# One S5 layer, four edits: state products over four quarters of TensorE, a contiguous tap table, whole-block turns, and layer-norm sums of one operand

## The chip, the cores and the metric

The kernel runs on one core of a Trainium2 chip. The metric is the time of one execution on the device, in microseconds. TensorE (PE) multiplies a stationary operand, loaded into its 128 by 128 array, with a moving operand whose columns stream through, and writes to PSUM; a matmul may use only half of the rows or columns of the array. VectorE (DVE), ScalarE (ACT) and GpSimd (POOL) work beside it, and SyncE (SP) issues the DMAs. Each engine takes its instructions in order.

## The reference

The program is a trunk of two layers over 1024 tokens of 1024 channels, in float32. Layer 0 is an RWKV-7 time mixer, layer 1 an S5 state-space layer; each is followed by a squared-ReLU MLP, and each of the four sub-layers by a layer norm of a scaled residual sum. Cut to what matters here:

```
def layer_norm(x, g, b):
    mu = mean(x);  var = mean(square(x - mu))
    return (x - mu) * rsqrt(var + LN_EPS) * g + b

def s5_mix(x, ...):            # 64 groups of 16 channels, 64 complex states each
    abar, bbar = discretised(a, log_dt, b)
    h[t] = abar * h[t-1] + bbar @ x[t]
    y[t] = real(c @ h[t]) + d * x[t]
    z = gelu(y) @ w_glu
    return z[:d] * sigmoid(z[d:])

for i in range(2):
    h = layer_norm(alpha * h + mixer_i(h))
    h = layer_norm(alpha * h + square(relu(h @ w1)) @ w2)
```

## The kernel before

The tokens are worked in two halves of 512 (H = 0 in the tiles hA, H = 1 in hB), each as eight tiles of 128 channels by 512 tokens. The dense products make up most of the time. Each weight tile is loaded (wraw, two buffers, L169), split into a high and a low part (whi on ScalarE, L148; wlo on VectorE, L149), and three matmuls of 512 columns (L188) make up one product. The two halves run against each other: while one is in its mixer, the dense products of the other half's MLP lie in between.

No order is written out around the change. A planner sets the order of the instructions of every engine when the program is built, from priorities, its own due times and the buffers that are free. So an edit in one place can move instructions elsewhere.

The S5 layer works eight tokens at a time (SL = 8), so that a half has NSC = 64 columns of states. The effect of the last tokens on the next ones is taken from a table of taps (tT, used as tt), the effect of the state from another (tC, used as tcm), and a third (tB, used as tb) brings inputs into the states. s5_tables builds the three into DRAM, at 1120 to 1270 us: for each of eight tiles f, VectorE and POOL expand the powers (L1133 to L1138), TensorE makes the taps (pk, L1151), ScalarE copies them into kpad, a buffer whose lower part holds zeros (L1155), and SP stores kpad into tT in two stores (L1159), each of which repeats the shifted taps for the eight steps.

s5(H, h) then runs for each half.

- Turn of the input, for four pairs of channel tiles f2: pu1 brings tokens onto partitions in 16 turns (L154 is a plain matmul with the identity, L156 a transpose), ScalarE copies them (u1), pu2 turns them once more per group of 16 channels (L1195), giving ug, and pbu brings them into the states hb (L1206).
- Scan: VectorE and POOL advance the states (L1216 to L1222).
- Outputs, again for four f2 (called rounds): the tap products (L1250, of ug with tt) and the state products (L1255, of hb with tcm) are summed in py, for the two parities par of the groups one after the other; ScalarE copies py into y1 (L1257), TensorE turns it back (pyt, L1263), VectorE adds the input (yg, one buffer, L1265), ScalarE takes the GELU (L1267), and SP stores to s_y (L1268). The tables of one round fill the four buffers of the tag tab.

In these products j, the tile in the pair, is the half of the array's columns; for the state products par is the half of its rows.

layer_norm is called seven times with the eight tiles h. Two partial sums are added up, TensorE sums over channels with a matrix of ones (pm, L865 and L866), VectorE subtracts the mean (L868), ScalarE squares and VectorE and POOL add the squares up in two sums sq0 and sq1 (L876), and pq sums both over channels (L880).

PSUM tiles come from four pools: pd (three, dense products), pl (one, tag l), pa (two, tag a) and pc (two, tag c).

Of the kernel before, what the change touches and what calls it, by code (L numbers as in the profile page):

```python
# [8 lines left out]
F32 = mybir.dt.float32  # L9
# [9 lines left out]
HT = 512  # L19
KT = 8  # L20
# [50 lines left out]
def trunk(ctx, tc, A):  # L71
# [90 lines left out]
    def wload(src, kt, n, key=None):  # L162

        step = 512 // n
        out = []
        for k0 in range(0, kt, step):
            kept = low.get((key, k0)) if key else None
            raw = wp.tile([128, step, n], F32, tag="wraw", name="wraw", bufs=2)
            SP.dma_start(raw, src[:, k0 : k0 + step])  # L169
# [12 lines left out]
        return out  # L182

    bulk, hops = [], []
    ST = getattr(nc, STE)
# [662 lines left out]
    def layer_norm(h, gi, H, split_out=True):  # L848
# [5 lines left out]
        def plt(name):  # L854
            return pl.tile([128, HT], F32, tag="l", name=name)
# [10 lines left out]
        PE.matmul(pm, ones_c, h[7], start=False, stop=True)  # L866
        for t in h:
            V.tensor_sub(t, t, pm)  # L868
        sa = [lt("sq0"), lt("sq1")]
        for k, t in enumerate(h):  # L870
            if k < 2:
                S.activation(sa[k], t, AF.Square)
            else:
                q = lt("sq", "m")
                S.activation(q, t, AF.Square)
                (G if k % 2 else V).tensor_add(sa[k % 2], sa[k % 2], q)  # L876
        pq = plt("pq")
        for t in range(4):
            for j in range(2):
                PE.matmul(pq[:, t : t + 1], sa[j][:, t * 128 : (t + 1) * 128], ones_c[:, 0:1], start=j == 0, stop=j == 1)  # L880
# [138 lines left out]

    SL = 8  # L1020
    NSC = HT // SL
    tT = dr.tile([KT, 128, 2, 512], F32, name="tT")
    tB = dr.tile([KT, 128, 4, 2, 128], F32, name="tB")
    tC = dr.tile([KT, 128, 4, 2, 128], F32, name="tC")

    def s5_tables():
# [75 lines left out]
        V.tensor_sub(ci, ci, tq)  # L1102
        V.tensor_mul(ci, ci, den)

        kpad = pp.tile([128, 16, 16, 4], F32, name="kpad")
        G.memset(kpad, 0.0)
        for f in range(KT):
            gs = slice(4 * f, 4 * f + 4)
            bc = pp.tile([128, 2, 2, 4, 16], F32, tag="bc", name="bc", bufs=1)
            SP.dma_start(bc, A["s5bc"][f])  # L1110
            bb = pp.tile([128, 2, 4, 16], F32, tag="bb", name="bb", bufs=1)
# [40 lines left out]
                                  ca[ps_, g2, ri, 0:8].rearrange("p t c -> p (t c)"), start=ri == 0, stop=ri == 1)  # L1152
            for par in range(2):
                ps_ = slice(64 * par, 64 * par + 16)
                S.copy(kpad[ps_, 8:].rearrange("p t c g -> p g (t c)"), p[ps_])  # L1155
            tv = tT[f].rearrange("(s c) two n -> two c s n", c=16)
            for par in range(2):
                src = kpad[64 * par : 64 * par + 16, 1:9].rearrange("p t c g -> p (t c g)")
                SP.dma_start(tv[par], bass.AP(src.tensor, src.offset, [src.ap[0], (64, SL), src.ap[1]]))  # L1159

            bs = pp.tile([128, 4, 2, 128], F32, tag="bs", name="bs", bufs=1)
            for hf in range(2):
# [10 lines left out]
    def s5(H, h):  # L1173
# [4 lines left out]
            V.tensor_copy(hb[:, :, :, 0], carry[0])  # L1178
        ug = []
        for f2 in range(4):  # L1180
            u1 = s5p.tile([128, 8, SL, 16], F32, tag="u1", name="u1", bufs=2)
            for s2 in range(2):
                p = pa.tile([128, 4, 128], F32, tag="a", name="pu1")
                for j in range(2):
                    src = h[2 * f2 + j].rearrange("p (c s) -> p c s", s=SL)
                    for s in range(4):
                        turn(p[64 * j : 64 * j + 64, s], src[:, :, SL - 1 - 4 * s2 - s], ident, j)
                S.copy(u1[:, :, 4 * s2 : 4 * s2 + 4].rearrange("p g s c -> p s g c"),
                       p.rearrange("p s (g c) -> p s g c", g=8))
            for j in range(2):  # L1190
                f = 2 * f2 + j
                ps_ = slice(64 * j, 64 * j + 64)
                p = pc.tile([128, HT], F32, tag="c", name="pu2").rearrange("p (g n) -> p g n", g=8)
                for g in range(8):
                    PE.transpose(p[:, g], u1[ps_, g].rearrange("p s c -> p (s c)"), ident[ps_, ps_])  # L1195
# [39 lines left out]
        for f2 in range(4):  # L1235
            y1 = s5p.tile([128, SL, 4, 2, 16], F32, tag="u1", name="y1", bufs=2)
            tabs = []
            for f in (2 * f2, 2 * f2 + 1):
                tt = s5p.tile([128, 2, 512], F32, tag="tab", name="tt", bufs=4)
                SP.dma_start(tt, tT[f])  # L1240
                tcm = s5p.tile([128, 4, 2, 128], F32, tag="tab", name="tcm", bufs=4)
                SP.dma_start(tcm, tC[f])
                tabs.append((f, tt.rearrange("p two (n g) -> p two g n", g=4), tcm))
            for par in range(2):
                qs = slice(64 * par, 64 * par + 64)
                p = pc.tile([128, HT], F32, tag="c", name="py").rearrange("p (g n) -> p g n", g=4)

                for g2 in range(4):
                    for j, (f, tv, tcm) in enumerate(tabs):
                        PE.matmul(p[64 * j : 64 * j + 64, g2], ug[f][:, 2 * g2 + par], tv[:, par, g2],  # L1250
                                  start=g2 == 0, stop=False, skip_group_check=True)
                for g2 in range(4):
                    for ri in range(2):
                        for j, (f, tv, tcm) in enumerate(tabs):
                            PE.matmul(p[64 * j : 64 * j + 64, g2], hb[qs, 4 * f + g2, ri, 0:NSC], tcm[qs, g2, ri],  # L1255
                                      start=False, stop=ri == 1, skip_group_check=True)
                S.copy(y1[:, :, :, par].rearrange("p t g c -> p g t c"), p.rearrange("p g (t c) -> p g t c", t=SL))  # L1257
            for j in range(2):
                f = 2 * f2 + j
                js = slice(64 * j, 64 * j + 64)  # L1260
                p = pa.tile([128, SL, NSC], F32, tag="a", name="pyt")
                for t in range(SL):
                    PE.transpose(p[:, t], y1[js, t].rearrange("p g r c -> p (g r c)"), ident[js, js])  # L1263
                y = s5p.tile([128, HT], F32, tag="yg", name="yg", bufs=1)
# [131 lines left out]
```

## Time and profile before

| | |
|---|---|
| median of three runs | 2739.15 us (2727.84 to 2743.22) |
| profiled execution | 2746.6 us, span 2744.8 us |
| mean granted TensorE clock | 0.961 of full speed |
| TensorE, VectorE, ScalarE, GpSimd busy | 95%, 66%, 42%, 23% of the span |
| building the S5 tables | about 1120 to 1270 us |
| S5 of the first half | about 1327 to 1545 us |
| S5 of the second half | about 1858 to 2075 us |

The profile is of one execution. A busy time is the time in which the engine had an instruction running. A row of a timeline gives start, length, engine, line and the number of instructions of that line in a row. A row of groups gives line, engine, operation, output from inputs, shape and count, then busy time in all and the mean of one in ns, then the idle time of the engine just before them and what ended it. For an fp32 matmul with a plain (not a transposing) operation the trace holds two records.

### The profile page before, as it was taken

How to read it: one execution, taken by the hardware profiler on the slowest of the kernel's cores; microseconds unless marked ns; L12 is line 12 of the kernel's file. 1: busy time of each engine (PE TensorE's matmuls, PEld its weight loads, DVE VectorE, ACT ScalarE, POOL GpSimd, SP SyncE). 2: the span in 40 equal slices, each digit the busy share in tenths (PEclk: the TensorE clock that was granted, in tenths of full speed). 3: DMA queues.
4: the chain of work that ended last, by engine and by line, in shares of the span. 5: the costliest groups of instructions: out<-in, count | busy, mean ns of one | idle time of the engine just before them, and what ended most of it. 6: DMA issues, size and time to landing. Idle time of an engine off the chain costs nothing.

```text
span 2744.8 us, 43807 instructions
## 1 busy us (share of the span) xinstructions
PE 2598.4 (95%) x16582; PEld 2089.9 (76%) x16582; DVE 1813.3 (66%) x3191; ACT 1154.8 (42%) x2038; POOL 630.6 (23%) x515
## 2 busy tenths in 40 slices
PE   7999979989899999989999999999999999999997
PEld 5778757678677777767876788778778887788886
DVE  7477677577786867997567553674855546755556
ACT  7455574544543333353532332434223324433334
POOL 3121542432442122342122000120220101210101
PEclk9989979999899999999999999999999999999998
DMA  4765455564223334545333533233343322333333
GB/s 146 235 214 175 151 164 156 178 203 142 81 86 88 93 92 148 141 129 163 100 112 127 174 95 100 81 96 112 103 164 110 96 96 81 119 96 96 96 96 100
DMA packets 215058, 345.90 MB, mean 126 GB/s; under 512 B 21184, under 2 KB 75584, under 8 KB 214848
## 3 DMA queue, kind: packets, MB, share of 16 engines
q1 hardware_dynamic: 214848, 343.10, 40.5%
q8 instruction: 131, 2.15, 0.3%
q14 instruction: 79, 0.65, 0.1%
HBM read 279.06 MB, written 63.96 MB: 125 GB/s over the span
## 4 chain that ended last, share of the span: by engine, by line
PE 44%; DVE 4%; issue 3%; DMA 1%; POOL 1%; ACT 1%; ACTq 0%; SPq 0%; DVEq 0%; POOLq 0%
PE d L188 39%; PE py L1250 1%; PE py L1255 1%; DVE wlo L149 1%; DMA wraw<-in_mw_dram 1%; PE pu L154 1%; PE pbu L1206 1%; POOL rl L975 1%; DVE hA L991 0%; DMA s_y<-yg 0%; DVE t L1218 0%; DVE hB L991 0%; ACT whi L148 0%; DVE sq L876 0%; PE pu L1195 0%
## 5 line engine op out<-in xcount | busy, mean ns | idle before, releaser
L148 ACT CAST whi<-wraw 128x512 fp32r<-128x512 f32 x668 | 413.5, 620 | 929.1 <-PE d L188 623.2
L149 DVE TENSOR_TENSOR wlo<-wraw,whi 128x512 fp32r<-128x512 f32 x668 | 500.6, 750 | 426.8 <-ACT whi L148 404.3
L188 PE MATMUL d<-qbuf,whi 128*128 128x512 f32 (+1 forms) x2112 | 657.0, 394 | 23.8 <-DVE hA L991 12.8
L188 PEld LDWEIGHTS d<-qbuf,whi 128*128 128x128 f32 x2112 | 391.8, 191 | 120.0 <-DVE hA L991 17.8
L188 PE MATMUL d<-qbuf,wlo 128*128 128x512 f32 (+1 forms) x1056 | 411.9, 392 | 10.7 <-DVE wlo L149 10.4
L975 POOL TENSOR_TENSOR rl<-rl 128x512 f32<-128x512 f32 x128 | 157.2, 1228 | 1094.5 <-ACT rl L974 1094.5
L188 PE MATMUL d<-oAh,whi 128*128 128x512 f32 (+1 forms) x960 | 390.9, 411 | 15.5 <-ACT ev L418 6.3
L188 PE MATMUL d<-oAl,whi 128*128 128x512 f32 (+1 forms) x960 | 387.5, 405 | 3.0 <-DVE oAl L149 2.8
L188 PE MATMUL d<-oAh,wlo 128*128 128x512 f32 (+1 forms) x960 | 386.5, 405 | 2.4 <-DVE wlo L149 2.3
L188 PE MATMUL d<-oBh,whi 128*128 128x512 f32 x704 | 279.2, 397 | 0.0
L188 PE MATMUL d<-oBh,wlo 128*128 128x512 f32 x704 | 278.7, 396 | 0.2 <-DVE wlo L149 0.2
L188 PE MATMUL d<-oBl,whi 128*128 128x512 f32 x704 | 277.1, 394 | 0.0
L188 PEld LDWEIGHTS d<-qbuf,wlo 128*128 128x128 f32 x1056 | 201.7, 191 | 56.5 <-DVE wlo L149 14.5
L188 PEld LDWEIGHTS d<-oAh,whi 128*128 128x128 f32 (+1 forms) x960 | 185.9, 194 | 62.2 <-ACT ev L418 8.4
L188 PEld LDWEIGHTS d<-oAh,wlo 128*128 128x128 f32 (+1 forms) x960 | 185.8, 194 | 44.4 <-DVE wlo L149 3.2
L188 PEld LDWEIGHTS d<-oAl,whi 128*128 128x128 f32 (+1 forms) x960 | 185.6, 194 | 43.1 <-DVE oAl L149 5.2
L991 DVE TENSOR_TENSOR hB<-hB,d 128x512 f32<-128x512 f32 (+1 forms) x256 | 165.0, 650 | 71.2 <-PE d L188 68.0
L991 DVE TENSOR_TENSOR hA<-hA,d 128x512 f32<-128x512 f32 x240 | 162.1, 682 | 64.4 <-PE d L188 62.1
L188 PEld LDWEIGHTS d<-oBh,wlo 128*128 128x128 f32 x704 | 132.9, 189 | 32.4 <-issue 2.0
L188 PEld LDWEIGHTS d<-oBl,whi 128*128 128x128 f32 x704 | 133.1, 189 | 29.9 <-issue 0.7
L188 PEld LDWEIGHTS d<-oBh,whi 128*128 128x128 f32 x704 | 133.1, 189 | 29.0 <-issue 1.2
L149 DVE TENSOR_TENSOR qbuf<-rl,qbuf 128x512 fp32r<-128x512 f32 x128 | 95.0, 742 | 73.5 <-ACT qbuf L148 73.5
(374 smaller groups left out, 3804.8 us busy)
## 6 DMA issues: line engine op xcount, KB each, us to landing
wraw<-in_mw_dram SPq DMA_DIRECT2D x520, 256.0 KB, 2.7
wraw<-in_glu_dram SPq DMA_DIRECT2D x64, 256.0 KB, 2.7
low<-wlo SPq DMA_DIRECT2D x52, 256.0 KB, 2.6
wlo<-low SPq DMA_DIRECT2D x52, 256.0 KB, 3.6
wraw<-in_wk_dram SPq DMA_DIRECT2D x32, 256.0 KB, 3.5
wraw<-in_wr_dram SPq DMA_DIRECT2D x32, 256.0 KB, 3.9
wraw<-in_wv_dram SPq DMA_DIRECT2D x32, 256.0 KB, 4.3
yl<-s_y SPq DMA_DIRECT2D x32, 256.0 KB, 3.1
```

The lines of the kernel that those rows point to most:

```text
L148: S.copy(hi, src)
L149: (e or V).tensor_sub(lo, src, hi.bitcast(F32))
L154: PE.matmul(out, x, idt, start=True, stop=True)
L188: bulk.append((PE.matmul(p, w, x, **kw).ins, x.shape[-1]))
L975: G.tensor_mul(r, r, r)
L991: V.tensor_add(z, z, p)
L1206: PE.matmul(p[qs, g2, ri], tb[:, g2, ri, qs], u[:, 2 * g2 + par], start=True, stop=True)
L1250: PE.matmul(p[64 * j : 64 * j + 64, g2], ug[f][:, 2 * g2 + par], tv[:, par, g2], start=g2 == 0, stop=False, skip_group_check=True)
L1255: PE.matmul(p[64 * j : 64 * j + 64, g2], hb[qs, 4 * f + g2, ri, 0:NSC], tcm[qs, g2, ri], start=False, stop=ri == 1, skip_group_check=True)
```

## The change

The lines of the changed kernel are some 6 to 20 higher than those before: the dense products are L196 and wraw's load L171; the tap products are L1262 (before L1250), the state products L1270 (L1255), the turn back L1280 (L1263), yg's store L1285 (L1268), the stores into tT L1170 (L1159).

The four quarters. One round now has two PSUM tiles, one per parity, from two pools (pc and pa), and the state products go through j and par in turn, so that four products in a row use the four quarters of the array. inorder ties each of them behind the one before. The turned outputs pyt move from the pool pa to pl.

The tap table. kpad and tT are laid out with the group g ahead of the taps, so that the columns of one group are contiguous (they stood 16 bytes apart). Each tile's taps go out in eight stores instead of two, and kpad is doubled.

The turns. pu1 now turns blocks of 128 tokens by 128 channels (eight transposes per f2, every fourth token a column); pu2 picks even and odd with a matrix sel of two interleaved halves of the identity, in 32 matmuls in place of 16 transposes.

The layer norms. The last tile is added on VectorE, so that pm is one matmul; sq0 and sq1 are added on VectorE, so that pq takes four matmuls and not eight.

```
+    sel = cp.tile([128, 2, 64], F32, name="sel")
+    V.tensor_copy(sel, ident.rearrange("p (n e) -> p e n", e=2))
...
+    def inorder(prods):
+        for x, y in zip(prods, prods[1:]):
+            tc.add_manual_dep(y.ins, x.ins.name, ...)
...
+        V.tensor_add(b2, b2, h[7])
         V.tensor_add(a, a, b2)
         pm = plt("pm")
-        PE.matmul(pm, ones_c, a, start=True, stop=False)
-        PE.matmul(pm, ones_c, h[7], start=False, stop=True)
+        PE.matmul(pm, ones_c, a, start=True, stop=True)
...
+        V.tensor_add(sa[0], sa[0], sa[1])
         pq = plt("pq")
         for t in range(4):
-            for j in range(2):
-                PE.matmul(pq[:, t : t + 1], sa[j][:, t * 128 : (t + 1) * 128], ones_c[:, 0:1], start=j == 0, stop=j == 1)
+            PE.matmul(pq[:, t : t + 1], sa[0][:, t * 128 : (t + 1) * 128], ones_c[:, 0:1], start=True, stop=True)
...
-    tT = dr.tile([KT, 128, 2, 512], F32, name="tT")
+    tT = dr.tile([KT, 128, 2, 4, 128], F32, name="tT")
...
-        kpad = pp.tile([128, 16, 16, 4], F32, name="kpad")
-        G.memset(kpad, 0.0)
+        kpads = [pp.tile([128, 4, 16, 16], F32, name=f"kpad{j}") for j in range(2)]
+        for kpad in kpads:
+            G.memset(kpad[:, :, 0:8], 0.0)
...
             for par in range(2):
-                src = kpad[64 * par : 64 * par + 16, 1:9].rearrange("p t c g -> p (t c g)")
-                SP.dma_start(tv[par], bass.AP(src.tensor, src.offset, [src.ap[0], (64, SL), src.ap[1]]))
+                for g2 in range(4):
+                    src = kpad[64 * par : 64 * par + 16, g2, 1:9].rearrange("p t c -> p (t c)")
+                    SP.dma_start(tv[par, g2], bass.AP(src.tensor, src.offset, [src.ap[0], (16, SL), src.ap[1]]))
...
-            for s2 in range(2):
+            for j in range(2):
                 p = pa.tile([128, 4, 128], F32, tag="a", name="pu1")
-                for j in range(2):
-                    src = h[2 * f2 + j].rearrange("p (c s) -> p c s", s=SL)
-                    for s in range(4):
-                        turn(p[64 * j : 64 * j + 64, s], src[:, :, SL - 1 - 4 * s2 - s], ident, j)
+                src = h[2 * f2 + j].rearrange("p (m s) -> p s m", s=4)
+                for s in range(4):
+                    PE.transpose(p[:, s], src[:, 3 - s], ident)
...
                 for g in range(8):
-                    PE.transpose(p[:, g], u1[ps_, g].rearrange("p s c -> p (s c)"), ident[ps_, ps_])
+                    for e in range(2):
+                        PE.matmul(p[64 * (1 - e) : 64 * (1 - e) + 64, g], u1[:, j, g].rearrange("p s c -> p (s c)"),
+                                  sel[:, e], start=True, stop=True)
...
+            pp = [r.tile([128, HT], F32, tag=t, name="py").rearrange("p (g n) -> p g n", g=4)
+                  for r, t in ((pc, "c"), (pa, "a"))]
+            ...
+            for g2 in range(4):
+                for ri in range(2):
+                    for j, (f, tv, tcm) in enumerate(tabs):
+                        for par in range(2):
+                            qs = slice(64 * par, 64 * par + 64)
+                            prods.append(PE.matmul(pp[par][64 * j : 64 * j + 64, g2], hb[qs, 4 * f + g2, ri, 0:NSC],
+                                                   tcm[qs, g2, ri], start=False, stop=ri == 1, skip_group_check=True))
+            inorder(prods)
...
-                p = pa.tile([128, SL, NSC], F32, tag="a", name="pyt")
+                p = pl.tile([128, HT], F32, tag="l", name="pyt").rearrange("p (t n) -> p t n", t=SL)
```

The planner's order in two places. A row gives line, operation, output from inputs, shape, and how many in a row. First TensorE in the outputs of the first half, in the kernel before: the end of one round's dense products (the d rows), the turn back of the round before (pyt), and the products of the next round.

```order
L188 MATMUL d<-oBh,wlo 128x512
L1250 MATMUL py<-tt,ug 64x128
L1263 MATMUL pyt<-ident,y_13970 128x64 x16
L1250 MATMUL py<-tt,ug 64x128 x7
L1255 MATMUL py<-tcm,hb 64x128
L1250 MATMUL py<-tt,ug 64x128 x5
L1255 MATMUL py<-tcm,hb 64x128 x15
L1250 MATMUL py<-tt,ug 64x128 x3
L1255 MATMUL py<-tcm,hb 64x128 x16
L188 MATMUL d<-oBh,whi 128x512
```

The same place in the changed kernel:

```order
L1280 MATMUL pyt<-ident,y_13958 128x64 x8
L1262 MATMUL py<-tt,ug 64x128 x14
L1270 MATMUL py<-tcm,hb 64x128 x13
L1280 MATMUL pyt<-ident,y_13958 128x64 x8
L1270 MATMUL py<-tcm,hb 64x128 x19
L1262 MATMUL py<-tt,ug 64x128 x2
L196 MATMUL d<-qbuf,whi 128x512 x2
```

The sixteen turns back of one round stood together and are now two times eight, the second amid the next state products; and the first two tap products of the round that follows stand directly behind the last state product, ahead of the round's dense products.

Second, SP's queue while the tables are built, before:

```order
L169 DMA wraw<-in_wo_dram 128x512
L1168 DMA tB<-bs 128x1024
L1144 DMA tC<-ca 1024x1x128
L169 DMA wraw<-in_wo_dram 128x512 x2
L1159 DMA tT<-kpad 16x8x512 x2
L1110 DMA bc<-in_s5bc_dram 128x256
```

The changed kernel there:

```order
L171 DMA wraw<-in_wo_dram 128x512
L1154 DMA tC<-ca 1024x1x128
L171 DMA wraw<-in_wo_dram 128x512 x2
L1170 DMA tT<-kpad_12861 16x8x128 x8
L1120 DMA bc<-in_s5bc_dram 128x256
```

Two stores per tile have become eight, in a row, between the loads of weights (wraw).

More of the change, by code (lines that the diff above doesn't have):

```diff
@@ L1239, in s5 @@
                 tt = s5p.tile([128, 2, 512], F32, tag="tab", name="tt", bufs=4)
-                SP.dma_start(tt, tT[f])
+                SP.dma_start(tt, tT[f].rearrange("p two g n -> p two (g n)"))
                 tcm = s5p.tile([128, 4, 2, 128], F32, tag="tab", name="tcm", bufs=4)
                 SP.dma_start(tcm, tC[f])
-                tabs.append((f, tt.rearrange("p two (n g) -> p two g n", g=4), tcm))
-            for par in range(2):
[L1245 to L1257, printed above, removed]
@@ new lines, in s5 @@
+                tabs.append((f, tt.rearrange("p two (g n) -> p two g n", g=4), tcm))
+            pp = [r.tile([128, HT], F32, tag=t, name="py").rearrange("p (g n) -> p g n", g=4)
[3 more added lines that the diff above has]
+                    for j, (f, tv, tcm) in enumerate(tabs):
+                        PE.matmul(pp[par][64 * j : 64 * j + 64, g2], ug[f][:, 2 * g2 + par], tv[:, par, g2],
+                                  start=g2 == 0, stop=False, skip_group_check=True)
@@ new lines, in s5 @@
+            prods = []
+            for g2 in range(4):
+                for ri in range(2):
+                    for j, (f, tv, tcm) in enumerate(tabs):
+                        for par in range(2):
+                            qs = slice(64 * par, 64 * par + 64)
+                            prods.append(PE.matmul(pp[par][64 * j : 64 * j + 64, g2], hb[qs, 4 * f + g2, ri, 0:NSC],
+                                                   tcm[qs, g2, ri], start=False, stop=ri == 1, skip_group_check=True))
@@ L1258, in s5 @@
+            inorder(prods)
+            for par in range(2):
+                S.copy(y1[:, :, :, par].rearrange("p t g c -> p g t c"), pp[par].rearrange("p g (t c) -> p g t c", t=SL))
             for j in range(2):
```

13 lines of the change are left out of this document (7 added, 6 removed).

## The prediction

> **What bounds the kernel now.** I read the engine totals and the chain of waits on the page, then the tables of busy time by stretch, then single stretches instruction by instruction.
>
> ```profile
> PE 2598.4 (95%) x16582; PEld 2089.9 (76%) x16582; DVE 1813.3 (66%) x3191; ACT 1154.8 (42%) x2038; POOL 630.6 (23%) x515
> PE 44%; DVE 4%; issue 3%; DMA 1%; POOL 1%; ACT 1%; ACTq 0%; SPq 0%; DVEq 0%; POOLq 0%
> ```
>
> TensorE is busy for 95% of the span, and the chain that ended last runs mostly over it; all other engines together are some 10%. Only 146 us of the 2744.8 us span have no matmul running (2744.8 − 2598.4). So TensorE time taken out of a stretch where it never idles comes off the end, unless something else takes its place. The next tables show the stretches that the change touches; columns are us, busy time (and count) of PE, PEld, DVE, ACT, POOL, the granted clock, the DMA share and GB/s.
>
> ```profile
> 1180.00:1200.00 20.00, 15.93 (x88) 11.78 (x86) 19.65 (x28) 9.03 (x14) 8.75 (x8) 0.96 0.53 128
> 1330.00:1405.00 75.00, 75.00 (x616) 60.56 (x615) 33.02 (x49) 30.24 (x53) 6.91 (x6) 1.00 0.38 119
> 1405.00:1480.00 75.00, 67.35 (x286) 51.23 (x285) 65.96 (x112) 20.06 (x34) 23.22 (x13) 0.97 0.29 89
> 1480.00:1545.00 65.00, 65.00 (x547) 49.40 (x546) 30.90 (x42) 23.02 (x38) 8.68 (x5) 0.99 0.64 219
> ```
>
> The S5 of the first half has three parts: turning the input (1330 to 1405), the scan (to 1480) and the outputs (to 1545). In the first and the last TensorE is busy for the whole stretch: dense products of the other half fill every gap. In the scan VectorE is the busiest engine. The second half's S5 repeats this around 1860 to 2075. The row of 1180 to 1200 stands for the building of the S5 tables: there VectorE works 19.65 of 20 us, and TensorE has 4 us of slack.
>
> **State products and tap products.** Rows of the output stretch, start, length, engine, line:
>
> ```profile
> 1481.22 3.55 PE L1255 MATMUL py<-tcm,hb 64*64 64x128 f32 x64
> 1494.38 2.01 PE L1250 MATMUL py<-tt,ug 128*64 128x128 f32 x16
> 345.90 0.71 PE L596 MATMUL pA<-AR,KB 64*128 64x128 f32 x8
> L1255 PE MATMUL py<-tcm,hb 64*64 64x128 f32 x512 | 32.5, 275 | 0.0
> L1250 PE MATMUL py<-tt,ug 128*64 128x128 f32 x256 | 40.4, 408 | 0.0
> L1166 PE MATMUL pb<-ident,bp 128*128 128x128 f32 x64 | 11.8, 290 | 4.9 <-DVE bp L1138 3.3 <-DVE bp L1135 1.4
> ```
>
> The trace has two records for each fp32 matmul, which I call passes. One L1255 pass lasts 275 ns, and 64 take 3.55 us, far less than 64 times that: passes go in pairs, the two column halves beside each other, (3.55 − 0.275) / 31 = 106 ns from pair to pair. The change puts four quarters in a row. If the two row halves overlap as well, 64 passes take 16 such steps and not 32; the 512 passes of the eight f2 rounds (four a half) lose 128 × 0.106 = −13.6 us. That row halves can overlap is seen in L596: eight passes, alternating between two row halves and two PSUM tiles, in 0.71 us; one after the other, 106 ns apart, they would need 7 × 0.106 + 0.27 = 1.01 us. The four quarters at once are in no row: the bounds are 0 (row halves do not overlap in this shape; a loss I exclude, since the same passes are issued) and −13.6. Since the new code, as L596, gives the row halves a PSUM tile each, I take −13.6.
>
> A tap pass (L1250) lasts 408 ns where passes of 128 columns otherwise last 275 to 290, and 16 take 2.01 us, that is 8 pairs (2.01 − 0.408) / 7 = 229 ns apart where L1255's need 106. What differs is the moving operand: a column every 16 bytes before, contiguous after. 128 pairs × (0.229 − 0.106) = −15.7; the other bound is 0, if the stride is not the cause. I take −15.7, since contiguous operands of 128 columns in the other two rows agree.
>
> **Turns.**
>
> ```profile
> 1327.37 1.03 PE L156 MATMUL pu<-ident,hA 128*64 128x128 f32 x8
> 1328.34 2.19 PE L154 MATMUL pu<-ident,hA 128*64 128x128 f32 x16
> 1330.46 0.73 PE L188 MATMUL d<-qbuf,whi 128*128 128x512 f32 x2
> ...
> 1331.26 0.62 PE L188 MATMUL d<-qbuf,whi 128*128 128x512 f32 x2
> 1331.72 0.39 PE L188 MATMUL d<-qbuf,wlo 128*128 128x512 f32 x1
> 1331.95 0.61 PE L188 MATMUL d<-qbuf,whi 128*128 128x512 f32 x2
> ...
> 1337.99 1.01 PE L1195 MATMUL pu<-ident,u 64*128 64x64 f32 x16
> 1338.94 0.50 PE L188 MATMUL d<-oBh,wlo 128*128 128x512 f32 x1
> 1343.73 2.09 PE L1206 MATMUL pbu<-ug,tb 128*64 128x64 f32 x64
> L156 PEld LDWEIGHTS pu<-ident,hA 128*64 128x64 f32 x32 | 3.8, 133 | 1.0
> L1166 PEld LDWEIGHTS pb<-ident,bp 128*128 128x128 f32 x64 | 7.9, 143 | 9.3 <-DVE bp L1138 4.7 <-ACT whi L148 1.7 <-issue 1.3
> ```
>
> First turn, per f2: 8 transposes and 8 matmuls (16 passes) from 1327.37 to 1330.46, 3.09 us. After: 8 whole transposes. At L156's pitch (1328.34 − 1327.37) / 8 = 0.121 us that is 0.97 us, and with 0.2 us for the change of shape 1.2: −1.9, times eight −15. They now load 128 columns and at a stride of 16 bytes, which no row has; L156 loads 64 at 32 bytes, as quickly (133 ns) as L1166 loads contiguous columns (143 ns). Bounds: −9.6 if the pitch doubled, −16. Second turn: 16 transposes in 0.95 us become 32 matmuls, 64 passes of L1206's shape, whose row gives 64 in 2.09 us: 8 × (2.02 − 0.95) = +8.6. The shape is L1206's, so ± 1. (Three dense products from 1331.26 to 1331.95 give 0.23 us each, used below.)
>
> The Trainium skill ("SBUF — State Buffer", section "Door 1: The DMA port swizzle") says that an access which leaves its 16-byte line each time pays a penalty. The tap row agrees (408 against 275 ns); the rule would double the new whole-block loads too, and the sum would be 5.4 us smaller, while L156's load at 32 bytes shows none, so the measurement decides.
>
> **Layer norms.**
>
> ```profile
> 1761.58 1.95 PE L880 MATMUL pq<-ones_c,sq 128*128 128x1 f32 x16
> L880 PE MATMUL pq<-ones_c,sq 128*128 128x1 f32 x112 | 16.5, 271 | 3.0 <-DVE sq L876 2.8
> L868 DVE TENSOR_TENSOR hA<-hA,pm 128x512 f32<-128x512 f32 x32 | 19.5, 679 | 0.7 <-PE pm L866 0.7
> L876 DVE TENSOR_TENSOR sq<-sq,sq 128x512 f32<-128x512 f32 x21 | 21.7, 1035 | 0.0
> L876 POOL TENSOR_TENSOR sq<-sq,sq 128x512 f32<-128x512 f32 x21 | 29.5, 1406 | 36.5 <-ACT sq L875 36.5
> ```
>
> Seven calls (112 passes / 16). The sums of squares lose 8 of 16 passes: (1.95 − 0.27) / 15 = 0.112 us each, −0.90. The mean loses one matmul of 512 columns, two passes at four times 106 ns: −0.85. Together −1.75 × 7 = −12.2. VectorE gets two more adds, 2 × 7 × 0.68 to 1.04 us = +10 to +15 on its own account. The second also makes VectorE wait for POOL's last add (1.4 us), with the mean's 8 subtractions and the next products' splits behind it. TensorE waits for the sums 3.0 us in all seven calls now, since dense products of the other half lie beside them; the adds lengthen that chain by 1.4 to 3.5 us a call and the shorter sums give 1.8 back. I take +3; bounds 0 and +12 (1.7 a call).
>
> **New waits in the outputs.**
>
> ```profile
> 1489.60 1.01 PE L1263 MATMUL pyt<-ident,y 64*128 64x64 f32 x16
> ...
> 1532.87 1.01 PE L1263 MATMUL pyt<-ident,y 64*128 64x64 f32 x16
> 1490.35 1.17 DVE L1265 SCALAR_TENSOR_TENSOR yg<-hA,pv,pyt 128x512 f32<-128x512 f32 x1
> 1494.35 1.19 DVE L1265 SCALAR_TENSOR_TENSOR yg<-hA,pv,pyt 128x512 f32<-128x512 f32 x1 [2.82 <-DMA s_y<-yg]
> L1257 ACT COPY y<-py 128x512 f32<-128x512 f32 x16 | 9.4, 586 | 33.8 <-PE py L1255 23.1 <-POOL t L1220 10.6
> DMA to landing us min/median/max: 3.8/4.4/6.2
> ```
>
> The last row is of the table tT (all its transfers). Two things come nearer to TensorE. First, the turned output goes to a pool of one buffer: the second eight transposes stand amid the next state products and need VectorE's sum of the first eight to be done, and the next f2 needs the second sum, which waits for yg's store (2.82 us above, one buffer). 4.0 us lie between the two sums above; between the transposes in the new order lie at most 14 tap and 13 state matmuls (1.5 + 0.7 us) and, next, 18 dense ones (4.1 us). Second, in the new order two tap products of the next f2 stand right behind the last state product, and their table's load can start only when the current taps are over, that is 32 state matmuls (1.75 us) and 8 transposes (0.5 us) earlier. A load takes 4.4 us, so TensorE waits 4.4 − 2.3 = 2.1 us, in the last two rounds of each half (the first two have their buffers early): 4 × 2.1 = +8. Before, 21 dense products (4.8 us) lay in between. With the sum's wait uncovered as well, 2 us more in each of eight rounds, it is +24; the lower bound is +3, loads at 3.8 us and half of it hidden.
>
> **Tables.**
>
> ```profile
> L1159 SPq DMA_DIRECT2D tT<-kpad x16: 320/362/1264, 1128.6 to 1268.9; - x16
> SPq L169 <- DVE wlo L149: 65.4, 28, 5.6
> L1155 ACT COPY kpad<-pk 16x512 f32<-16x512 f32 x16 | 17.1, 1072 | 6.3 <-PE pk L1151 6.1
> ```
>
> Each tile's two stores become eight: 6 × 0.362 = +2.2 us on SP's queue, 17 us for eight tiles, ahead of weight loads (wraw, two buffers). In 1120 to 1270 SP itself waited 65.4 us for a free wraw buffer, so most is hidden; if that cover were gone it would be +17 and more. I take +4, bounds 0 and +17. The copy ahead of the stores gets a contiguous target (1072 ns now, 586 ns in L1257's row for as much data a partition), off the path. The doubled kpad and the one copy of sel I cost at nothing: VectorE's queue at the start and POOL's have slack (23% busy).
>
> **Sum.** −13.6 − 15.7 − 15 + 8.6 − 12.2 + 3 + 8 + 4 = −33 us. The profiled execution took 2746.6 us (span 2744.8), which would become about 2714; it lies 7.4 us above the median of the three runs, 2739.15, so against the median I predict 2706 us. 0.5%, about what these runs can tell from no change, is 13.7 us: faster means below 2725.5, slower above 2752.8.
>
> **Rivals.**
> Row halves do not overlap: state products keep 106 ns a pair; L596 speaks against it, its different shape for it. 2706 + 14 = 2720.
> The stride is not the tap pass's cost: 2706 + 16 = 2722. The equal 275 to 290 ns of both other rows speak against it.
> The outputs are paced by something else than TensorE: a round ((1532.87 − 1489.60) / 3 = 14.4 us) has four table loads of 512 KB, two yg stores and the chain through one pyt buffer, with a DMA share of 0.64 already. If the round stays at its length, the 29 us of products come back as idle time: −33 + 29 − 8 (the wait counted above) = −12, so 2727, and up to 2740 with waits of the upper bounds.
> Slower: the 64 stores hold the weight loads back. SP works its queue in order, so a store that waits for ACT's copy or for an earlier transfer holds wraw behind it, and TensorE has only two of them in hand while VectorE is full. To reach 2752.8 the wait must eat the gain and 14 more, 47 us, that is 6 us a tile beyond the 0.5 in the sum; the stores' own issue is 2.2, so each tile must also wait for about one landing (4.4 us). The 65.4 us that SP spends waiting speak against it.
>
> **How the numbers follow.** Forecast, 0.48, alone 2693 to 2720 (the bounds of turns, norms and waits). No overlap 0.12, no gain by contiguity 0.05, outputs paced by others 0.15, stores in the way 0.10, and 0.10 for the order changing elsewhere, either way. The range reaches from 2688 (waits at their lower bounds, −9, and 8 of run to run spread) to 2738, which holds the first three cases and most of the fourth and leaves out 0.18. Faster: 0.48 + 0.11 + 0.05 + 0.03 + 0.04 = 0.71; slower 0.07 + 0.03 = 0.10; the rest 0.19.
>
> **What would show it.** State products: 64 passes in about 1.8 us instead of 3.55. Taps: passes near 280 ns, 16 in 1.1 us. First turns: eight in 1.0 us; second: 64 in 2.0. The norms' sums: 8 passes in 1.0. TensorE idle at the first tap products of a round, about 2 us, released by the load of tt. TensorE busy about 2550 us. I am wrong if the four quarters still take 106 ns a pair, if the idle time in the outputs is above 15 us, or if TensorE idles more than now (4 of 20 us) while the tables are built.

## The result, and the profile after

The changed kernel took 2709.23 us (median of four runs, 2705.1 to 2714.34), the kernel before 2737.76 on the same occasions: a ratio of 0.9901, 95% interval 0.9875 to 0.9926, or 20 to 34 us less; the difference of the medians is 28.5 us where 33 were forecast. Medians leave out executions that were disturbed as a whole, such as one of 6511.5 us of the kernel with the old tap table. The profiled execution has a span of 2707.5 us. Engine totals and the chain that ended last, from its page, and the chain of a second execution of the same kernel:

```profile
PE 2541.4 (94%) x16768; PEld 2059.2 (76%) x16768; DVE 1830.7 (68%) x3206; ACT 1144.4 (42%) x2038; POOL 622.4 (23%) x516
PE 62%; DVE 18%; DMA 8%; issue 5%; ACT 5%; POOL 2%; SPq 0%; ACTq 0%; DVEq 0%; POOLq 0%
PE 43%; DVE 9%; DMA 4%; issue 2%; ACT 1%; POOL 0%; SPq 0%; ACTq 0%; DVEq 0%; POOLq 0%
```

TensorE is busy 57.0 us less (2598.4 − 2541.4), the span is 37.3 us shorter, so some 20 us of new idle time have come. The shares of the chain can't be compared: they add up to 100% here, to 59% in the second execution and to 54% in the kernel before, so the chain was followed over different parts of the span. VectorE's 18% and 9% are of one and the same kernel. The outputs of the first half, as a timeline and then as groups, and below them TensorE's busy time in the outputs of the first and of the second half:

```profile
1454.50 1.98 PE L1270 MATMUL py<-tcm,hb 64*64 64x128 f32 x64
1462.74 1.96 PE L1262 MATMUL py<-tt,ug 128*64 128x128 f32 x28
1470.02 1.11 PE L1262 MATMUL py<-tt,ug 128*64 128x128 f32 x4 [2.42 <-DMA tt<-tT]
...
1484.49 1.12 PE L1262 MATMUL py<-tt,ug 128*64 128x128 f32 x4 [2.56 <-DMA tt<-tT]
L1270 PE MATMUL py<-tcm,hb 64*64 64x128 f32 x512 | 17.7, 274 | 0.0
L1262 PE MATMUL py<-tt,ug 128*64 128x128 f32 x256 | 22.4, 284 | 9.2 <-DMA tt<-tT 9.2
1453.00:1511.00 58.00, 53.02 (x530) 42.58 (x529) 29.76 (x35) 22.21 (x39) 9.57 (x6) 0.91 0.66 231
1970.00:2025.00 55.00, 50.42 (x531) 40.27 (x530) 27.65 (x35) 19.89 (x36) 10.56 (x7) 0.97 0.60 206
```

64 state passes take 1.98 us, before 3.55: (1.98 − 0.274) / 15 = 114 ns for four. A tap pass lasts 284 ns, before 408; 14 pairs in a row are (1.96 − 0.284) / 13 = 129 ns apart, before 229. And TensorE waits 2.42 and 2.56 us for a table, at the place and for the reason that the order had shown. The last two rows give 5.0 + 4.6 = 9.6 us of idle time in the two output stretches, where the kernel before had none. The turns and the norms' sums, and four contiguous blocks turned in a row in the kernel before (L1166):

```profile
1324.94 1.11 PE L1198 MATMUL pu<-ident,hA 128*128 128x128 f32 x8
1325.81 0.48 PE L196 MATMUL d<-oBh,wlo 128*128 128x512 f32 x1
1331.04 2.08 PE L1205 MATMUL pu<-sel,u 128*64 128x64 f32 x64
1749.44 0.95 PE L888 MATMUL pq<-ones_c,sq 128*128 128x1 f32 x8
L1198 PEld LDWEIGHTS pu<-ident,hA 128*128 128x128 f32 x32 | 5.0, 206 | 0.5
1132.86 0.60 PE L1166 MATMUL pb<-ident,bp 128*128 128x128 f32 x4
```

Eight whole-block turns take 0.87 us up to the next product (predicted 1.2, before 3.09); the second turns 2.08 us, as predicted.

More new idle time lies around the layer norms. Three stretches without any S5 work, between the tables and the first S5, between the two S5, and after the second to the last norms, in the kernel before and then in the changed one (columns as in the prediction):

```profile
1272.00:1330.00 58.00, 57.14 (x267) 46.40 (x267) 43.81 (x66) 25.37 (x43) 12.32 (x10) 1.00 0.41 132
1536.00:1860.00 324.00, 322.45 (x1425) 262.57 (x1424) 192.00 (x288) 120.35 (x206) 47.80 (x43) 1.00 0.32 96
2063.00:2677.00 614.00, 610.02 (x2662) 497.79 (x2661) 347.54 (x525) 213.58 (x363) 74.50 (x69) 0.99 0.33 99
```

```profile
1235.00:1323.00 88.00, 81.91 (x355) 65.96 (x354) 63.24 (x94) 38.45 (x67) 22.17 (x16) 0.98 0.34 116
1511.00:1842.00 331.00, 324.05 (x1422) 264.20 (x1421) 197.16 (x295) 120.93 (x206) 48.51 (x44) 1.00 0.29 95
2025.00:2640.00 615.00, 608.11 (x2664) 496.91 (x2663) 353.27 (x534) 216.01 (x368) 76.07 (x71) 1.00 0.30 99
1253.68 1.24 ACT L150 CAST whi<-wraw 128x512 fp32r<-128x512 f32 x2 [9.46 <-DMA wraw<-in_mw_dram]
1254.35 0.50 PE L196 MATMUL d<-oAh,whi 128*128 128x512 f32 x1 [4.23 <-ACT whi L150]
```

Length less TensorE's busy time gives 0.9 + 1.6 + 4.0 = 6.4 us before and 6.1 + 7.0 + 6.9 = 19.9 after: 13.5 us more. The first stretch is not alike in the two (58 and 88 us), and 4.2 of its 6.1 us are one wait for a weight tile whose load came late (the last two rows); the other two stretches are alike and went from 5.5 to 13.8 us. What a norm looks like from VectorE and TensorE, timeline of the changed kernel:

```profile
1743.40 0.68 DVE L151 TENSOR_TENSOR wlo<-wraw,whi 128x512 fp32r<-128x512 f32 x1
1744.01 1.27 DVE L999 TENSOR_TENSOR hB<-hB,d 128x512 f32<-128x512 f32 x2
1745.20 0.68 DVE L885 TENSOR_TENSOR sq<-sq,sq 128x512 f32<-128x512 f32 x1
1745.81 0.67 DVE L999 TENSOR_TENSOR hB<-hB,d 128x512 f32<-128x512 f32 x1
1744.73 0.73 PE L196 MATMUL d<-qbuf,whi 128*128 128x512 f32 x2 [0.95 <-DVE hB L999]
```

VectorE works without a gap there; its queue holds the norm's adds, the splits of weights (wlo) and the sums that take dense products out of PSUM (hB, L999). TensorE's next dense product waits 0.95 us for such a sum. The new add (L885) stands in that same queue.

### The profile page after: what moved, and what is told of

Read it like the earlier page. It is cut to its first block, busy times and chain, and to the rows that moved or that the text cites. A ratio compares the mean times of both kernels' runs of the same rounds, so it can differ in the third digit from the quotient of the medians.

```text
span 2707.5 us, 44238 instructions
## 1 busy us (share of the span) xinstructions
PE 2541.4 (94%) x16768; PEld 2059.2 (76%) x16768; DVE 1830.7 (68%) x3206; ACT 1144.4 (42%) x2038; POOL 622.4 (23%) x516
## 4 chain that ended last, share of the span: by engine, by line
PE 62%; DVE 18%; DMA 8%; issue 5%; ACT 5%; POOL 2%; SPq 0%; ACTq 0%; DVEq 0%; POOLq 0%
PE d L196 55%; DVE wlo L151 3%; PE pA L604 2%; DMA wraw<-in_mw_dram 1%; DMA yl<-s_y 1%; DVE hA L999 1%; DMA s_y<-yg 1%; ACT whi L150 1%; DVE t L1229 1%; DMA ldsg<-s_sg 1%; DVE sq L884 1%; DVE hB L999 1%; PE pbu L1217 1%; PE pu L1205 1%; DVE xh L649 1%
## 5 line engine op out<-in xcount | busy, mean ns | idle before, releaser
L196 PE MATMUL d<-qbuf,whi 128*128 128x512 f32 (+1 forms) x2112 | 656.4, 393 | 31.4 <-DVE hA L999 15.2
L196 PEld LDWEIGHTS d<-qbuf,whi 128*128 128x128 f32 x2112 | 391.5, 191 | 126.9 <-DVE hA L999 23.4
L196 PE MATMUL d<-qbuf,wlo 128*128 128x512 f32 (+1 forms) x1056 | 409.5, 390 | 9.3 <-DVE wlo L151 9.1
L196 PE MATMUL d<-oAh,whi 128*128 128x512 f32 (+1 forms) x960 | 391.4, 411 | 21.9 <-ACT ev L426 6.5
L983 POOL TENSOR_TENSOR rl<-rl 128x512 f32<-128x512 f32 x128 | 145.1, 1133 | 1090.4 <-ACT rl L982 1071.3
L196 PE MATMUL d<-oAl,whi 128*128 128x512 f32 (+1 forms) x960 | 386.4, 404 | 1.1 <-DVE oAl L151 1.1
L196 PE MATMUL d<-oAh,wlo 128*128 128x512 f32 (+1 forms) x960 | 385.8, 404 | 1.0 <-DVE wlo L151 1.0
L196 PE MATMUL d<-oBh,wlo 128*128 128x512 f32 x704 | 278.4, 396 | 1.5 <-DVE wlo L151 1.5
L196 PE MATMUL d<-oBh,whi 128*128 128x512 f32 x704 | 279.8, 397 | 0.0
L196 PE MATMUL d<-oBl,whi 128*128 128x512 f32 x704 | 275.8, 392 | 0.0
L196 PEld LDWEIGHTS d<-qbuf,wlo 128*128 128x128 f32 x1056 | 201.2, 191 | 54.0 <-DVE wlo L151 12.8
L196 PEld LDWEIGHTS d<-oAh,whi 128*128 128x128 f32 (+1 forms) x960 | 185.8, 194 | 67.5 <-ACT ev L426 8.6
L196 PEld LDWEIGHTS d<-oAh,wlo 128*128 128x128 f32 (+1 forms) x960 | 185.9, 194 | 42.4 <-DVE wlo L151 2.0
L196 PEld LDWEIGHTS d<-oAl,whi 128*128 128x128 f32 (+1 forms) x960 | 186.2, 194 | 39.8 <-DVE oAl L151 2.2
L999 DVE TENSOR_TENSOR hB<-hB,d 128x512 f32<-128x512 f32 (+1 forms) x256 | 165.1, 652 | 65.8 <-PE d L196 62.7
L999 DVE TENSOR_TENSOR hA<-hA,d 128x512 f32<-128x512 f32 x240 | 162.4, 682 | 45.6 <-PE d L196 43.5
L196 PEld LDWEIGHTS d<-oBh,wlo 128*128 128x128 f32 x704 | 132.9, 189 | 33.4 <-DVE wlo L151 2.1
L196 PEld LDWEIGHTS d<-oBl,whi 128*128 128x128 f32 x704 | 132.8, 189 | 29.1 <-issue 0.2
L196 PEld LDWEIGHTS d<-oBh,whi 128*128 128x128 f32 x704 | 133.0, 189 | 28.5 <-issue 0.8
```

What stands on the lines that cost most here:

```text
L196: bulk.append((PE.matmul(p, w, x, **kw).ins, x.shape[-1]))
L983: G.tensor_mul(r, r, r)
L999: V.tensor_add(z, z, p)
```

## The experiments

All times are medians; each set ran beside the kernel before, and ratios are to that kernel. Two runs of the changed kernel gave 2709.23 and 2712.97. The sets ran on different chips, so the distances of medians from these two are rough. By ratios, against 0.9902 (the mean of the changed kernel's two), the run with row halves one after the other, the old tap table, the old turns and the old norms lie 6, 7, 10 and 17 us above it, and the intervals of the first two overlap the changed kernel's.

**The changed kernel again**

> The changed kernel unaltered, beside the others of this set: 2709 to 2712 on the chip where the kernel before takes 2738 to 2741. It says how far medians of equal kernels lie apart.

2712.97 us, ratio 0.9903 (0.9887 to 0.9919). Medians of one kernel lie up to 4 us apart, so differences below some 5 us say nothing here.

**Row halves one after the other**

```
-                    for j, (f, tv, tcm) in enumerate(tabs):
-                        for par in range(2):
+            for par in range(2):                # outermost
+                for g2 ... for ri ... for j ...
```

> The changed kernel with the state products of one parity after the other, so that only pairs of column halves stand in a row; the two PSUM tiles and all else stay. If row halves overlap and TensorE's own work sets the time, 64 passes take 3.5 us again instead of 2.0 and the kernel takes 13.6 us more than 2709, about 2723. Rival: the outputs are paced by the table loads; the products before each round's first taps are then 1.75 us longer and the wait of 2.2 to 2.6 us for tt shrinks by as much in four rounds, so only 13.6 - 7 = 7 us more, about 2716. If row halves did not overlap, no difference: 2709.

2721.08 us, ratio 0.9923 (0.9905 to 0.994): 8 to 12 us above the changed kernel by medians. Timeline and groups, and last a row of another line in the kernel before, used further down:

```profile
1461.59 3.34 PE L1270 MATMUL py<-tcm,hb 64*64 64x128 f32 x64
1479.08 0.65 PE L1262 MATMUL py<-tt,ug 128*64 128x128 f32 x4 [1.69 <-DMA tt<-tT]
L1270 PE MATMUL py<-tcm,hb 64*64 64x128 f32 x512 | 28.0, 273 | 0.0
L1262 PE MATMUL py<-tt,ug 128*64 128x128 f32 x256 | 22.8, 284 | 7.2 <-DMA tt<-tT 7.2
421.08 1.71 PE L596 MATMUL pA<-AR,KB 64*128 64x128 f32 x16
```

The order of the passes alone makes 3.34 us of 1.98: the four quarters do run at once. (With the row halves the two PSUM tiles also come one after the other here, so this run does not say which of the two the overlap needs.) Busy time of the state products is 10.3 us more (28.0 − 17.7), and the wait for tt is 2 us less, between the two theories: part of the gain of the quarters is lost to waiting for the tables.

**The tap table as before**

```
-    tT = dr.tile([KT, 128, 2, 4, 128], F32, name="tT")
+    tT = dr.tile([KT, 128, 2, 512], F32, name="tT")
...  (one kpad [128, 16, 16, 4], two stores a tile)
```

> The changed kernel with the tap table as before: group last, columns 16 bytes apart, two stores a tile, one kpad. If the stride costs, tap passes are 408 ns again and the eight rounds take 15.7 us more; the six stores a tile fewer give back what they cost (4 by the prediction): about +12, 2721. Rival: the eight stores cost as much as the contiguous reads gain: 2709. Second rival: the stride is not the cause, tap passes stay near 284 ns: about 2705.

2724.18 us, ratio 0.9926 (0.9905 to 0.9946): 11 to 15 us above the changed kernel by medians, 7 by ratios. This agrees with the stride, but alone does not show it, and no tap pass was read from a trace of this kernel. The other traces say it more plainly: a tap pass lasts 408 ns on the mean in the three other kernels with the old table (the kernel before, and that kernel with eight stores and with the new norms, below), and 275 to 299 in the changed kernel and all its variants with the contiguous one.

**The turns as before**

```
-                src = h[2 * f2 + j].rearrange("p (m s) -> p s m", s=4)
-                for s in range(4):
-                    PE.transpose(p[:, s], src[:, 3 - s], ident)
+                    turn(p[64 * j : 64 * j + 64, s], src[:, :, SL - 1 - 4 * s2 - s], ident, j)
...  (and pu2 as 16 transposes)
```

> The changed kernel with the first and second turn of the input as before. By the trace the first turn lost 20.1 us of TensorE's time and the second gained 8.6, so +11.5 us, about 2721. Rival: these savings were given back in the scan behind them, where VectorE is the busiest engine: 2709.

2723.44 us, ratio 0.9938 (0.9921 to 0.9956): 10 to 14 us more, the first theory. The turns' gain was not given back. (The groups of the first turn add up to 28.3 us before and 9.8 after, 18.5 less and not 20.1.)

**Eight stores a tile in the kernel before**

```
+                for q in range(4):
+                    src = kpad[64 * par : 64 * par + 16, 1 + 2 * q : 3 + 2 * q]...
+                    SP.dma_start(tv[par][:, :, 128 * q : 128 * q + 128], ...)
```

> The kernel before with each of the two tap stores of a tile cut in four (128 columns each, runs of 512 bytes), so eight a tile; the table's layout stays. By the prediction +4 (0 to 17), so 2739 to 2755, about 2743. Rival of the prediction: the stores hold the weight loads back, 6 us a tile: +47, about 2785.

2739.74 us, ratio 0.9992 (0.998 to 1.0003): no cost. SP's waits while the tables are built:

```profile
SPq L169 <- DVE wlo L149: 41.7, 24, 5.5
SPq L1160 <- ACT kpad L1155: 10.0, 4, 4.7
```

SP had waited 65.4 us for free weight buffers there and now waits 41.7: the 48 more stores took their time out of this slack.

**Layer norms: the changed ones in the kernel before, and the old ones in the changed kernel**

```
+        V.tensor_add(b2, b2, h[7])
...
+        PE.matmul(pm, ones_c, a, start=True, stop=True)
...
+        V.tensor_add(sa[0], sa[0], sa[1])
...  (four matmuls into pq)
```

> The kernel before with the layer norms of the changed one alone. By the prediction -9 us, about 2730. By what the changed kernel lost without them (23 us at the medians) -20, about 2719: then TensorE's share of the norms was put too low. Rival: the two adds hold VectorE's chain up where the norms stand alone: 2739.

> The changed kernel with the layer norms as before (two matmuls for the mean, eight for the squares, two adds fewer on VectorE). By the prediction TensorE gets 12.2 us more and VectorE's chain gives 3 back: +9, about 2718; by the trace's TensorE time it would be up to +15, 2724. Rival: the adds on VectorE cost as much as the matmuls they replace, since TensorE then waits for the sums: 2709 or less.

In the kernel before, the new norms alone take 2742.28 us, ratio 1.0009 (0.9997 to 1.0022): no gain. The page, and the three stretches around the norms:

```profile
PE 2583.8 (94%) x16512; PEld 2084.0 (76%) x16512; DVE 1837.6 (67%) x3205; ACT 1154.8 (42%) x2038; POOL 624.5 (23%) x515
1249.00:1341.00 92.00, 84.79 (x368) 68.36 (x366) 65.85 (x98) 41.62 (x72) 22.12 (x16) 0.96 0.35 110
1544.00:1870.00 326.00, 319.84 (x1409) 261.23 (x1408) 196.91 (x293) 121.88 (x207) 47.67 (x43) 1.00 0.30 96
2071.00:2678.00 607.00, 600.06 (x2629) 490.28 (x2628) 347.64 (x525) 212.96 (x362) 74.89 (x69) 1.00 0.33 99
PE d L188 <- ACT whi L148: 4.3, 1, 4.3
PE d L188 <- DVE hB L991: 4.1, 3, 1.7
PE d L188 <- DVE hA L991: 5.5, 5, 1.6
```

TensorE is busy 14.6 us less (2598.4 − 2583.8), and over the whole span its idle time is 2745.5 − 2583.8 = 161.7 us where it was 146.4, 15.3 more. What TensorE saved came back as waiting. In these three stretches the idle time is 7.2 + 6.2 + 6.9 = 20.3 us, 13.9 more than before, though the first is again longer than its counterpart. The last three rows, one of each stretch, say what ended the most of it. VectorE's sums, which take dense products out of PSUM, ended 9.8 us of the waits in all three, where it was 3.2 in the kernel before (L989 and L991); one late weight tile ended 4.3. So VectorE's sums are behind about half of the new waits.

The other way round the numbers do not fit: the changed kernel with the old norms takes 2732.01, ratio 0.9964 (0.9947 to 0.9981), 19 to 23 us more, although its idle time around the norms falls to 7.1 us. Of the 22.3 us between its profiled execution and the changed kernel's (spans 2729.8 and 2707.5), 18.7 are TensorE's busy time and only 3.6 idle time: what it no longer waits around the norms, it waits elsewhere. Its outputs and its tables have got worse: idle time in the tables is 152.00 − 130.61 = 21.4 us (changed kernel 142.00 − 126.62 = 15.4), in the two output stretches 16.2 (9.6). The second row is the sum over the three stretches around the norms (981.00 − 973.86 = 7.1), the last is of the changed kernel's tables:

```profile
PE 2560.0 (94%) x16838; PEld 2069.1 (76%) x16838; DVE 1822.0 (67%) x3192; ACT 1144.2 (42%) x2038; POOL 630.8 (23%) x516
sum 981.00, PE 973.86 PEld 793.57 DVE 570.06 ACT 349.01 POOL 134.81; mean PE 324.62 PEld 264.52 DVE 190.02 ACT 116.34 POOL 44.94
1117.00:1269.00 152.00, 130.61 (x746) 98.61 (x743) 140.24 (x218) 58.60 (x102) 60.91 (x43) 0.96 0.55 145
1466.00:1526.00 60.00, 52.84 (x532) 41.39 (x532) 29.08 (x37) 21.55 (x37) 11.60 (x8) 0.94 0.66 224
1991.00:2052.00 61.00, 52.01 (x536) 41.09 (x535) 31.34 (x40) 21.23 (x38) 11.55 (x7) 0.97 0.56 186
1093.00:1235.00 142.00, 126.62 (x729) 95.61 (x730) 137.61 (x212) 51.64 (x89) 53.94 (x40) 0.96 0.57 154
```

The planner starts the tables there at 1117 us and not at 1093, and the rest of the order moves with them. To part this from the norms, each half of the edit was undone by itself.

> The changed kernel with the mean as before (two matmuls, one add fewer on VectorE in each norm), the squares as changed. TensorE gets 4 us more in all. If VectorE is what TensorE waits for in the norms (13 us of new waits there, from two adds), half of these go: -3, about 2709 where the changed kernel takes 2712. Rival: TensorE's time is the price and the waits stay: +4, 2716. Second rival: the order that the planner finds matters more than either, and most of the 20 us of the kernel without both edits come from this one.

> The changed kernel with the sums of squares as before (eight matmuls, no add of the two sums on VectorE), the mean as changed. TensorE gets 11 to 12 us more. If VectorE is what TensorE waits for, about 7 us of the waits go: +4, about 2716. Rival: only TensorE's time counts: +12, 2724.

With the old mean 2713.03 us (0.9892, 0.9869 to 0.9916), with the old squares 2715.29 (0.991, 0.9889 to 0.9932). Neither differs from the changed kernel by more than runs differ. TensorE is busy 8.5 and 14.1 us more than in the changed kernel:

```profile
PE 2549.9 (94%) x16782; PEld 2059.6 (76%) x16782; DVE 1820.4 (67%) x3199; ACT 1146.3 (42%) x2038; POOL 627.3 (23%) x516
PE 2555.5 (94%) x16824; PEld 2067.5 (76%) x16824; DVE 1828.2 (67%) x3199; ACT 1146.8 (42%) x2038; POOL 632.1 (23%) x516
```

So neither half's saving on TensorE shows as time by itself, and the 20 us of both together are more than the two halves sum to. Either the two act together or the order that the planner finds makes the difference; no run parts these. VectorE's sums end 9.5 us of TensorE's waits around the norms in the changed kernel, 8.9 with the old mean, 8.9 with the old squares and 3.5 with both old: the waits too go only when both are undone.

**The add of the two sums on POOL**

```
-        V.tensor_add(sa[0], sa[0], sa[1])
+        G.tensor_add(sa[0], sa[0], sa[1])
```

> The changed kernel with the add of the two sums of squares on POOL in place of VectorE (1.3 us there, 0.68 on VectorE; VectorE no longer waits for POOL's last add). If VectorE's queue is what holds the dense products in the norms, some 5 us of waits go: about 2707. Rival: the norm's own chain sets the time and it becomes 0.6 us longer in seven calls: +4, 2716.

2717.73 us, ratio 0.9909 (0.9886 to 0.9932): not to be told from the changed kernel. TensorE's waits for VectorE's sums around the norms are 9.0 us, 9.5 with the add on VectorE, so this one add in VectorE's queue does not make them by itself. Whether the length of the norm's chain does stays open.

**Taps later**

```
+                        if back:
+                            inorder([back[f2 - 1], tap])   # behind the first turn back of the round before
```

> The changed kernel with the tap products of a round tied behind the first turn back of the round before, so that the round's dense products (about 4 us) lie between the last state product and the first tap. If TensorE's wait for tt (9.2 us in five places) is a cost of the order alone, it goes and the time falls by 9, to about 2700. Rival: the outputs are paced by the loads and the one turned-output buffer, so the wait only moves to the next products: 2709.

2712.04 us, ratio 0.9899 (0.9882 to 0.9917): no gain. TensorE's wait for tt:

```profile
PE py L1263 <- DMA tt<-tT: 5.3, 2, 3.0
```

From 9.2 to 5.3 us only. The second tap table of a round stands in SP's queue behind a state table, whose buffer is free only after the state products. So the loads were put in another order too:

**Taps later, and tap tables loaded first**

```
+            tts = []
+            for f in (2 * f2, 2 * f2 + 1):
+                tt = s5p.tile(...); SP.dma_start(tt, tT[f]...); tts.append(tt)
+            for f, tt in zip(..., tts):
+                tcm = s5p.tile(...); SP.dma_start(tcm, tC[f])
```

> The kernel with the late taps, and the two tap tables of a round loaded ahead of the two state tables, so that no tap load stands behind a load that waits for the state products. If the rest of TensorE's waits for tt (5.3 us) came from that order of SP's queue, they go: 4 to 5 us below the kernel with late taps alone, 9 below the changed kernel, about 2702. Rival: the round is paced by the four loads of 512 KB themselves, and the state products then wait for tcm instead: 2712.

2708.92 us, ratio 0.9887 (0.9868 to 0.9905), the lowest of all, but inside the interval of the changed kernel. TensorE's wait has changed its name:

```profile
PE py L1276 <- DMA tcm<-tC: 6.7, 5, 2.8
```

The wait for tt is gone and one of 6.7 us for tcm has come. This is the rival: four table buffers hold one round, each is free only after the round's products, and the shorter the products, the less lies over the loads. A kernel with more table buffers was not run.

## Why the prediction was right, point by point

The time, 2709.2 for 2706, came out inside the forecast case, and the mechanisms of the outputs and turns were those forecast. That it came within 3 us is in part luck: the norms gave 9 us less than their terms and the waits cost 1.6 more, while the state products, taps, first turns and tables together came out 10 us better.

- *State products, −13.6.* Busy time of the groups went from 32.5 to 17.7 us, −14.8. All four quarters at once, the unknown of the prediction, were shown by the run with pairs, which lost 10.3 us of TensorE time by the order of the passes alone. The row of L596 that spoke for them was a favourable one: three other rows of that line have 16 passes in 1.71 us (one stands last in the rows of the run with pairs), that is (1.71 − 0.27) / 15 = 96 ns a pass, little overlap. So the full −13.6 was less sure than the chosen row made it.
- *Taps, −15.7.* Busy time 40.4 to 22.4, −18.0, more than by the row. Pairs are 129 ns apart, not 106, which gives 128 × (0.229 − 0.129) = −12.8. The taps also stand in longer runs now, with fewer changes of shape; that the rest comes from this was not measured apart.
- *Turns, −15 and +8.6.* The first: 8 × (3.09 − 0.87) = −17.8, beyond the bound of −16. The stride of 16 bytes in the stationary operand did not double the pitch: (1.11 − 0.28) / 7 = 0.119 us, against (0.60 − 0.29) / 3 = 0.103 for contiguous blocks. The load itself does take longer, 206 ns on the mean against 143 (L1166), but the loads overlap: eight of them are 1.65 us, and the eight passes take 1.11. So the Trainium skill's rule on 16-byte lines ("SBUF — State Buffer", section "Door 1: The DMA port swizzle") fits the moving operand of the taps, and of these transposes the length of the load but little of the pitch; L156's load of 64 columns at 32 bytes, 133 ns, shows no penalty at all. The second: 16.7 us of busy time for 8.1, +8.6.
- *Layer norms, −12.2 and +3.* Here a step failed: "the adds lengthen that chain by 1.4 to 3.5 us a call and the shorter sums give 1.8 back. I take +3; bounds 0 and +12". TensorE saved 14.6 us in the run with the norms alone, and 15.3 of idle time came, more than the bound of +12. I had taken the small idle time in front of the sums (3.0 us in seven calls) as a sign that the norms are covered by dense products. They are, but those dense products themselves began to wait: about half of the new waits are for VectorE to take earlier products out of PSUM, the rest for a late weight tile and others. In the kernel before, the net is 0, not −9. In the changed kernel it is not settled: each half undone costs nothing that can be told, both together 17 to 23 us. The sum below takes 0; with 17 or more it would not fit the time.
- *Waits in the outputs, +8.* 9.6 us of idle time in the two output stretches, none before, 9.2 of it for tt, at the predicted places, the last two rounds of each half, and about the predicted length (2.42 and 2.56 in the first half for 2.1). The buffer of the turned outputs cost 0.3 us. The upper bound, 24, was far off.
- *Tables, +4.* 0, by the run with eight stores; the cover was named (SP's wait for weight buffers) and is what took the cost.

The measured terms give −14.8 − 18.0 − 17.8 + 8.6 + 0 + 9.6 + 0 = −32, against −28 to −37 between medians and between profiled executions. Two slips of the working changed nothing: the low end of the range adds up to 2706 − 9 − 8 = 2689, not 2688, and the chain whose other engines are "some 10%" covers only 54% of the span. Of the rivals, quarters that do not overlap and a stride that costs nothing fell by the rows of the changed kernel; stores in the way fell by the run of their own; pacing by the tables is there at a third of its price, and the last two runs did not get it back by order while one round fills the buffers.

## What to carry to other kernels

A kernel that is 95% TensorE is not bound by TensorE everywhere: price an edit by the stretch in which it lies. Where VectorE works without a gap and also empties PSUM, a matmul less can be worth nothing, as the norms in the kernel before were. When products get faster, look at the loads which had room only because the products were slow; here they give back about a third of the gain of these products, and the two reorderings that were run only moved the wait. Where a planner orders the program, undoing one edit does not measure it: the edits undone one by one sum to 49 to 64 us by medians and to some 40 by ratios, and the change is worth 28.

## What the runs showed of the hardware that was not expected

fp32 passes of 64 by 64 run in all four quarters of the array at once at 114 ns for four of 128 columns; a pair of column halves took 106 ns in the kernel before and (3.34 − 0.27) / 31 = 99 ns in the run with pairs. The first 700 us, which hold none of the changed code, were not equal between single executions: TensorE's busy time there was 635.29 us in the kernel before, and 639.38 and 634.91 in two executions of the changed kernel, which have one and the same order:

```profile
0.00:700.00 700.00, 635.29 (x5491) 517.21 (x5493) 477.74 (x972) 395.11 (x726) 219.67 (x193) 0.92 0.55 174
0.00:700.00 700.00, 639.38 (x5525) 522.63 (x5526) 478.24 (x980) 395.04 (x728) 219.21 (x193) 0.92 0.54 175
0.00:700.00 700.00, 634.91 (x5500) 516.24 (x5501) 475.28 (x974) 394.25 (x727) 221.77 (x193) 0.92 0.55 174
```

One execution of a kernel runs ahead of another by that much before the change begins, which is part of the scatter of single profiled executions and of the 37 us between the two spans.
